# Matmul with rotary embedding on one core: two more pairs of tiles turned on VectorE, and another order of SyncE's loads

## The chip, the core and the metric

The kernel runs on one core of a Trainium2 chip. A core has five engines with their own instruction streams: TensorE (PE, matrix products; PEld in the profile is its weight load), VectorE (DVE), ScalarE (ACT), GpSimd (POOL) and SyncE (SP), which only starts transfers here. They meet through semaphores. Products land in PSUM; everything else lies in SBUF. Transfers between the chip's main memory and SBUF are started by SyncE, ScalarE or GpSimd, each with a queue of its own, and all queues are served by the same sixteen DMA engines.

The metric is the time of one execution in device microseconds; less is better. Before the change the median of 3 runs was 150.48 us (150.37 to 150.66).

## What is computed

```python
batch, seq, hidden, n_heads = (16, 512, 768, 12)      # x: 16 x 512 x 768, weight: 768 x 768
...
y = np.matmul(x, weight)
y = y.reshape(batch, seq, n_heads, head_dim)           # head_dim = 64
...
out1 = y1 * cos1 - y2 * sin1                           # y1, y2: halves of each head
out2 = y2 * cos2 + y1 * sin2
out = np.concatenate([out1, out2], axis=-1)
```

All inputs and the output are float32. The kernel multiplies in float16 and adds up in float32.

## The kernel before

**Tiles and groups.** The 8,192 rows of x are 64 tiles of 128 rows. Four tiles of four different batches that share their rows of cos and sin form a group; there are 16 groups (0 to 15), and tile i is in group i // 4. A group has two halves of two tiles each; a half is named (group, 0) or (group, 1). `NTILE` is 64, `QB` is 4 and `LAST` is 15.

**From x to the product.** PE needs each tile with the contraction along the partitions, so every tile must be transposed. There are two ways.

- A *plain* tile: `load` (L209) brings 128 rows of 3,072 bytes to one of ten buffers `xs` on SyncE's queue; `cast` on ScalarE makes float16 (`xc`, L189); PE transposes it with the identity into PSUM in 12 small products (`turn_rows`, L270); ScalarE copies the result to SBUF (`xt`, L189).
- A *block pair*: two tiles of a half go together, and PE doesn't transpose. `load_quarter` (L224) fetches four quarters, each 32 partitions by 8 rows by 192 values, so in rows of 768 bytes, already spread as the transposed layout needs. VectorE then turns blocks of 32 x 32 (`turn_pair`, L298, a STREAM_TRANSPOSE into `xp`). A pair marked "pool" is loaded by GpSimd's queue, which casts on the way (`xh`). A pair marked "sp" is loaded by SyncE in float32 (one of three buffers `xb`), and ScalarE casts the whole pair (`cast_pair`, L189, into one of two buffers `xd`).

`BLOCKS` (L140 to L142) lists the block pairs: the second halves of groups 4 to 13, ten pairs, "pool" in even groups and "sp" in odd ones.

**From product to output.** PE multiplies with the weight in row halves of 64 partitions (`walk` and `one`, L359) into six PSUM banks: three for a half of a group. VectorE multiplies each finished stretch with cos and sin at once (`rope`, L416; a half has one product of 128 x 1024 and one of 128 x 2048 results, both into `tq` or into the weight's former buffer `w_raw`), GpSimd adds the two parts (`add`, L442) into `ov`, and the result is stored from ScalarE's queue, at the end also from SyncE's (`store`, L474). Groups 14 and 15 go in smaller stretches; in the last one PE, VectorE and ScalarE take some additions.

**Order.** Each engine's order is written out by the loop over tiles (i from 4 to 63). At tile i, ScalarE casts up to five tiles ahead (`casts`, `C_AHEAD`), PE transposes up to three tiles ahead (`turns`, `T_AHEAD`), VectorE turns pairs whose first tile is less than four ahead (`bturns`), GpSimd issues loads up to 20 ahead (`pool_loads`). Every engine takes its instructions strictly in this order, so a wait holds all that stands behind it on that engine.

SyncE's order is the list `fetch`. `pump` issues from it as long as a buffer is free by the plan's count: a tile load needs one of the ten `xs`, a pair's first quarter one of the three `xb`. Before, the quarters of an "sp" pair are entered one by one behind plain tiles from the group ahead of the pair on:

```python
for i in range(QB, NTILE):
    if soon and i >= max(2, soon[0][0] - 1) * QB:
        quarters += [(soon[0], q) for q in (0, 2, 1, 3)]
```

Of the kernel before, what the change touches and what calls it, by code (L numbers as in the profile page):

```python
# [108 lines left out]
def kernel(  # L109
# [23 lines left out]
    QB = 4  # L133
    NG = B * SB // QB
    NTILE = QB * NG
# [4 lines left out]
    BLOCKS = {}  # L140
    for g in range(4, 14):
        BLOCKS[g, 1] = "pool" if g % 2 == 0 and g >= 4 else "sp"  # L142

    def sbuf(name, shape, dt):
        return nc.alloc_sbuf_tensor(name, shape, dt).ap()
# [50 lines left out]
    def pair_of(i):  # L196
        return i // QB, (i % QB) // 2

    def is_block(i):
        return pair_of(i) in BLOCKS  # L200
# [293 lines left out]
        out=sin_sb, in_=sin.rearrange("(p r) d -> p r d", r=SB)), writes=["sin"], dma="ov3_1536")  # L494


    fetch, quarters = [], []
    soon = [p for p in sorted(BLOCKS) if BLOCKS[p] == "sp"]
    for i in range(QB, NTILE):
        if soon and i >= max(2, soon[0][0] - 1) * QB:  # L500
            quarters += [(soon[0], q) for q in (0, 2, 1, 3)]
            soon.pop(0)
        if not is_block(i):
            fetch.append(i)
            if quarters:
                fetch.append(quarters.pop(0))
        elif quarters and quarters[0][0] == pair_of(i):
            fetch.append(quarters.pop(0))
    fetched = [0]
    xs_used, xb_used = [0], [0]  # L510
    xs_sent, xb_sent = [4], [0]
# [1 line left out]
    def pump():  # L513

        while fetched[0] < len(fetch):
            j = fetch[fetched[0]]
            if isinstance(j, int):
                if xs_sent[0] - xs_used[0] >= NX:
                    return
                load(j)  # L520
                xs_sent[0] += 1
            else:
                if j[1] == 0:
                    if xb_sent[0] - xb_used[0] >= NB:
                        return
                    xb_sent[0] += 1
                load_quarter(*j)
            fetched[0] += 1
# [45 lines left out]
    for c in CHUNKS[3:5]:  # L574
# [6 lines left out]
    do("dve", lambda eng: eng.tensor_scalar_mul(  # L581
        out=csn[:, 1, :, HD:D], in0=sin_sb[:, :, 0:HD], scalar1=-1.0),
        reads=["sin", "csn1", "cos"], writes=["csn"])
    assert not quarters
    pump()

    rows_on = [False]
# [42 lines left out]
    for g in range(LAST):  # L630
        for h in (0, 2):
            i = QB * (g + 1) + h
            q = (g, h * H, (h + 2) * H, "act")
# [4 lines left out]
            elif g < LAST - 2:  # L638
                i = QB * (LAST - 2) + 2 * (g - LAST + 4) + h // 2
            else:  # L640
                q = q[:3] + ("sp",)
# [22 lines left out]
    for i in range(QB, NTILE):  # L664
        g, s = divmod(i, QB)
# [13 lines left out]
        for n, p in enumerate(pieces(g, s)) if i >= ROWS else ():  # L679
            a, z, _, bank = p  # L680
# [66 lines left out]
```

## Time and profile before

| | us |
|---|---|
| median of 3 runs | 150.48 |
| the profiled execution, its own time | 150.94 |
| its span, first to last instruction | 149.1 |
| busy in the span: DVE / ACT / POOL | 126.0 / 77.9 / 123.2 |
| PE's transposes in row halves, 38 tiles in 456 products, busy | 15.4 |
| DVE's transposes of pairs: 5 from `xh`, 5 from `xd` | 6.2, 4.8 |
| ScalarE's pair casts, 5 | 8.2 |
| median from issue to landing: tile load / SyncE's quarter | 15.7 / 18.0 |

The profile is of one execution; its span leaves out the start and the end of the launch, so it is compared with that execution's own time. An engine's row gives the time it was busy. The chain of waits follows the work that ended last back through what released it. In the timeline the first column is the start and the second the duration of one or several like instructions; the brackets give the idle time ahead of them and who ended it. The share of the DMA engines can be above 1, because the records of packets on one engine overlap.

### The profile page before, as it was taken

What the parts mean: (1) busy time and instruction counts of PE and PEld (TensorE: products, weight loads), DVE (VectorE), ACT (ScalarE), POOL (GpSimd) and SP (SyncE); (2) the same over time, 40 slices, a digit from 0 to 9 for tenths busy, and PEclk for the clock granted to TensorE, in tenths of its full rate; (3) what the DMA queues carried; (4) which work ended last, traced back from release to release, by engine and by line L of the source; (5) the groups of instructions that cost most, each with busy time, mean ns of one, the idle gap of its engine ahead of it and who ended that gap; (6) DMA issues with size and microseconds to landing.
All of it is one profiled execution on the core that took longest, in us unless ns stands there. A gap on an engine that the chain in (4) does not pass through costs nothing.

```text
span 149.1 us, 4412 instructions
## 1 busy us (share of the span) xinstructions
PE 141.2 (95%) x1948; PEld 116.0 (78%) x1948; DVE 126.0 (84%) x96; ACT 77.9 (52%) x93; POOL 123.2 (83%) x72
## 2 busy tenths in 40 slices
PE   6759999999999999999999999999999999999990
PEld 2325568889888889888888888888888888864870
DVE  0244998884999999899999998999989998898990
ACT  3444698877761833547261915275263817764200
POOL 1000389999999999999999999779895999999990
PEclk9999999999999999999999999999999999999998
DMA  4999999999999999999999999999999999985574
GB/s 122 356 401 401 400 401 399 271 366 324 329 350 339 327 339 356 271 368 349 348 358 367 380 324 357 368 403 323 388 412 411 413 406 405 394 328 218 222 294 160
DMA packets 27555, 51.27 MB, mean 344 GB/s; under 512 B 7184, under 2 KB 13072, under 8 KB 27536
## 3 DMA queue, kind: packets, MB, share of 16 engines
q1 hardware_dynamic: 14736, 28.05, 54.2%
q10 hardware_dynamic: 7360, 20.97, 35.5%
q0 software_dynamic: 5440, 1.97, 10.7%
q8 instruction: 15, 0.25, 0.6%
q14 instruction: 4, 0.03, 0.1%
HBM read 27.79 MB, written 25.17 MB: 355 GB/s over the span
## 4 chain that ended last, share of the span: by engine, by line
PE 85%; DVE 6%; DMA 5%; SPq 1%; issue 1%; DVEq 0%
PE py L359 70%; PE py L334 8%; PE pt L270 5%; DMA w_raw<-in_weight_dram 5%; DVE tq L416 5%; SPq L209 1%; PE pt L255 1%; SPq L231 1%; DVE xs L416 1%; DVE w_sb L189 0%; DVE ov L442 0%; DVEq L57 0%; SPq L742 0%; SPq L119 0%
## 5 line engine op out<-in xcount | busy, mean ns | idle before, releaser
L442 POOL TENSOR_TENSOR ov<-tq 128x1536 f32<-128x1536 f32 (+3 forms) x32 | 76.4, 2412 | 19.4 <-DVE tq L416 19.2
L416 DVE TENSOR_TENSOR tq<-py,csn 128x1024 f32<-128x1024 f32 (+2 forms) x49 | 74.5, 1552 | 4.7 <-PE py L359 3.6
L359 PE MATMUL py<-w_sb,xt 64*128 64x512 f16 (+1 forms) x816 | 77.9, 323 | 0.0
L359 PEld LDWEIGHTS py<-w_sb,xt 64*128 64x128 f16 x816 | 59.2, 94 | 8.4 <-DVE tq L416 0.4
L189 ACT COPY xt<-pt 128x768 f16<-128x768 f16 x42 | 33.5, 799 | 51.7 <-PE pt L270 50.5
L359 PE MATMUL py<-w_sb,xp 64*128 64x512 f16 (+1 forms) x480 | 47.6, 323 | 0.0
L189 ACT CAST xc<-xs 128x768 f16<-128x768 f32 x44 | 38.8, 906 | 9.0 <-DMA xs<-in_x_dram 8.8
L359 PEld LDWEIGHTS py<-w_sb,xp 64*128 64x128 f16 x480 | 35.4, 94 | 4.5
L416 DVE TENSOR_TENSOR w_raw<-py,csn 128x1024 f32<-128x1024 f32 (+1 forms) x21 | 35.1, 1674 | 4.3 <-POOL w_raw L691 2.1
L442 POOL TENSOR_TENSOR ov<-w_raw 128x1536 f32<-128x1536 f32 (+2 forms) x13 | 35.1, 2718 | 2.0 <-DVE w_raw L416 1.8
L334 PE MATMUL py<-w_sb,xt 128*128 128x256 f16 (+2 forms) x132 | 20.1, 302 | 1.9 <-DVE w_sb L189 1.9
L334 PEld LDWEIGHTS py<-w_sb,xt 128*128 128x128 f16 x132 | 11.6, 98 | 8.1 <-DVE w_sb L189 3.3
L270 PEld LDWEIGHTS pt<-ident,xc 64*128 64x128 f16 x456 | 14.8, 95 | 1.7 <-ACT xc L189 0.6
L270 PE MATMUL pt<-ident,xc 64*128 64x64 f16 x456 | 15.4, 190 | 0.0
L224 POOL DMA_DIRECT2D xh<-in_x_dram x20 | 11.6, 588 | 0.0
L189 ACT CAST xd<-xb 128x1536 f16<-128x1536 f32 x5 | 8.2, 1638 | 0.0
L189 DVE CAST w_sb<-w_raw 128x768 f16<-128x768 f32 x6 | 3.4, 560 | 4.4 <-DMA w_raw<-in_weight_dram 4.4
L298 DVE STREAM_TRANSPOSE xp<-xh 128x768 f32<-128x768 f32 x5 | 6.2, 1237 | 0.0
L536 PE MATMUL py<-cold 128*128 128x512 f16 x12 | 4.4, 528 | 1.4 <-DVE cold L479 1.4
L189 DVE COPY xt<-pt 128x768 f16<-128x768 f16 x2 | 1.1, 558 | 4.8 <-PE pt L255 4.8
L298 DVE STREAM_TRANSPOSE xp<-xd 128x768 f32<-128x768 f32 x5 | 4.8, 969 | 0.0
L536 PEld LDWEIGHTS py<-cold 128*128 128x128 f16 x12 | 1.4, 129 | 3.5 <-issue 1.9
(21 smaller groups left out, 15.7 us busy)
## 6 DMA issues: line engine op xcount, KB each, us to landing
out_dram<-ov ACTq DMA_DIRECT2D x26, 768.0 KB, 9.0
xs<-in_x_dram SPq DMA_DIRECT2D x44, 384.0 KB, 15.7
xb<-in_x_dram SPq DMA_DIRECT2D x20, 192.0 KB, 18.0
out_dram<-ov SPq DMA_DIRECT2D x4, 768.0 KB, 3.7
w_raw<-in_weight_dram SPq DMA_DIRECT2D x6, 384.0 KB, 7.8
xh<-in_x_dram POOLq DMA_DIRECT2D x20, 96.0 KB, 14.5
out_dram<-ov SPq DMA_DIRECT2D x1, 384.0 KB, 2.3
out_dram<-ov ACTq DMA_DIRECT2D x1, 384.0 KB, 2.3
```

The costliest lines, as they stand in the source:

```text
L189: eng.copy(out=o, in_=i_) if e == "act" else eng.tensor_copy(out=o, in_=i_)
L209: do(e, lambda eng: eng.dma_start(out=xs_b[k], in_=x[b].rearrange("(p r) h -> r p h", r=SB)[r]), writes=[f"xs{k}"], dma=f"xs{k}")
L224: do(e, lambda eng: eng.dma_start(out=dst[ts(q, R)], in_=src[r, q]), writes=[f"{name}q{q}"], dma=name)
L231: do(e, lambda eng: eng.dma_start(out=w_raw[:, t, h], in_=wv[t, h]), writes=[f"wr{t}{h}"], dma=f"ov{t}_0" if h else f"xb{t}")
L255: do("pe", lambda eng: eng.transpose(pt[:, t, h, :], src[:, t, h, :], ident), reads=[f"xc{c}", "ident"], writes=[f"pt{k}"], tick=(t, h) == ...
L270: do("pe", lambda eng: eng.transpose(pts[r][:, t, h, :], src[rows, t, h, :], ident[rows, rows]), reads=[f"xc{c}", "ident"], writes=[f"pt{r ...
L298: do("dve", lambda eng: eng.transpose(out=dst, in_=src), reads=rd, writes=[f"xp{z}"])
L334: do("pe", lambda eng: eng.matmul(ps, get(t, h), w_sb[:, t, h, a - s * H : z - s * H], start=start, stop=stop), reads=[key, f"w{t}{h}"], w ...
L359: do("pe", lambda eng: eng.matmul(py[:, a:z], get(t, h)[rows], w_sb[rows, t, h, a - s * H : z - s * H], start=start, stop=not opens and en ...
L416: do("dve", lambda eng: eng.tensor_tensor(out=tq.rearrange("p j (h d) -> p j h d", d=D), in0=ps.rearrange("p (h d) -> p h d", d=D) .unsque ...
L442: do(adder, lambda eng: eng.tensor_tensor(out=ov_b[o][:, ds(c0, w)].rearrange("p (h t d) -> p h t d", t=2, d=HD), in0=tq[:, 0].rearrange(" ...
L536: do("pe", lambda eng: eng.matmul(py[:, ts(b, 512)], cold[:, 0:P], cold, start=True, stop=warmed[0] < WARM - 6), reads=["cold"], writes=[f ...
```

## The change

Two pairs become block pairs, the first halves of groups 9 and 12, that is tiles 36, 37, 48 and 49; both are "sp". In these two groups all four tiles are now in block pairs. And `fetch` is built anew: the plain tiles in order, and each quarter of an "sp" pair right behind one of the last four plain tiles ahead of the pair.

```diff
     for g in range(4, 14):
         BLOCKS[g, 1] = "pool" if g % 2 == 0 and g >= 4 else "sp"
+    for g in (9, 12):
+        BLOCKS[g, 0] = "sp"
...
-    fetch, quarters = [], []
-    soon = [p for p in sorted(BLOCKS) if BLOCKS[p] == "sp"]
-    for i in range(QB, NTILE):
-        if soon and i >= max(2, soon[0][0] - 1) * QB:
-            quarters += [(soon[0], q) for q in (0, 2, 1, 3)]
-            soon.pop(0)
-        if not is_block(i):
-            fetch.append(i)
-            if quarters:
-                fetch.append(quarters.pop(0))
-        elif quarters and quarters[0][0] == pair_of(i):
-            fetch.append(quarters.pop(0))
+    plain = [i for i in range(QB, NTILE) if not is_block(i)]
+    fetch = [(i, i) for i in plain]
+    for gh in sorted(BLOCKS):
+        if BLOCKS[gh] == "sp":
+            behind = [i for i in plain if i < gh[0] * QB + 2 * gh[1]][-4:]
+            fetch += [(i + 0.5, (gh, q)) for i, q in zip(behind, (0, 2, 1, 3))]
+    fetch = [what for _, what in sorted(fetch, key=lambda p: p[0])]
...
-    assert not quarters
```

From tile 28 on SyncE's order is then (Q is a quarter, named by its pair):

```
before: 28 Q(7,1) 29 Q(7,1) 32 Q(9,1) 33 Q(9,1) 36 Q(9,1) 37 Q(9,1) 40 Q(11,1) 41 Q(11,1) 44 Q(11,1) 45 Q(11,1) 48 Q(13,1) 49 Q(13,1) 52 Q(13,1) 53 Q(13,1) 56 ...
after:  28 Q(7,1) Q(9,0) Q(9,1)  29 Q(7,1) Q(9,0) Q(9,1)  32 Q(9,0) Q(9,1)  33 Q(9,0) Q(9,1)
        40 Q(11,1) Q(12,0)  41 Q(11,1) Q(12,0)  44 Q(11,1) Q(12,0) Q(13,1)  45 Q(11,1) Q(12,0) Q(13,1)  52 Q(13,1)  53 Q(13,1)  56 ...
```

## The prediction

> **What bounds the kernel now.** I read the busy shares first, then the stretches of the span with the DMA share, then the chain of waits, then ScalarE's and VectorE's own order in time.
>
> ```profile
> PE 141.2 (95%) x1948; PEld 116.0 (78%) x1948; DVE 126.0 (84%) x96; ACT 77.9 (52%) x93; POOL 123.2 (83%) x72
> ```
>
> The stretches (columns: length, then busy time of PE, PEld, DVE, ACT, POOL, granted clock, DMA share, GB/s):
>
> ```profile
> 24.00:60.00 36.00, 36.00 (x573) 31.84 (x571) 31.76 (x19) 22.69 (x29) 35.71 (x22) 1.00 1.13 337
> 60.00:94.00 34.00, 34.00 (x502) 30.14 (x499) 32.22 (x21) 16.50 (x20) 33.54 (x18) 1.00 1.12 347
> 94.00:124.00 30.00, 30.00 (x442) 26.52 (x438) 28.98 (x20) 15.10 (x17) 25.98 (x9) 1.00 1.04 392
> ```
>
> PE has no gap from 24 to 124 us, so PE sets the pace. But the DMA share is above 1: the sixteen DMA engines are full all that time, and the loads have no lead to give away. ScalarE's order and the chain show it for tiles 44 and 45 (casts at 92.52 and 94.03, PE's transposes of the same tiles at 97.58 and 99.68):
>
> ```profile
> 92.52 0.90 ACT L189 CAST xc<-xs 128x768 f16<-128x768 f32 x1
> 94.03 0.91 ACT L189 CAST xc<-xs 128x768 f16<-128x768 f32 x1 [0.60 <-DMA xs<-in_x_dram]
> 97.85 0.80 ACT L189 COPY xt<-pt 128x768 f16<-128x768 f16 x1 [2.92 <-PE pt L270]
> 98.55 1.64 ACT L189 CAST xd<-xb 128x1536 f16<-128x1536 f32 x1
> ...
> 100.07 0.81 ACT L189 COPY xt<-pt 128x768 f16<-128x768 f16 x1
> ```
>
> ```profile
> 97.58 0.16 PE pt L270 x9
> 97.75 0.03 PE py L359
> 97.78 0.03 PE pt L270
> 97.80 1.88 PE py L359 x18
> 99.68 0.19 PE pt L270 x10
> ```
>
> Tile 45's cast waits for its load (0.60 us); what still hides that is the time from the end of the cast (94.94) to PE's first transpose of the tile (99.5 in the order of PE): 4.6 us.
>
> The other near bounds are DVE and POOL:
>
> ```profile
> 101.11 1.23 DVE L416 TENSOR_TENSOR tq<-py,csn 128x1024 f32<-128x1024 f32 x1
> 102.25 0.97 DVE L298 STREAM_TRANSPOSE xp<-xd 128x768 f32<-128x768 f32 x1
> 103.15 5.58 DVE L416 TENSOR_TENSOR tq<-py,csn 128x2048 f32<-128x2048 f32 x3
> 109.26 1.23 DVE L416 TENSOR_TENSOR w_raw<-py,csn 128x1024 f32<-128x1024 f32 x1 [0.54 <-PE py L359]
> 110.41 1.23 DVE L298 STREAM_TRANSPOSE xp<-xh 128x768 f32<-128x768 f32 x1
> 111.56 2.25 DVE L416 TENSOR_TENSOR w_raw<-py,csn 128x2048 f32<-128x2048 f32 x1
> ```
>
> ```profile
> 113.95 3.47 POOL L442 TENSOR_TENSOR ov<-w_raw 128x1536 f32<-128x1536 f32 x1 [1.51 <-DVE w_raw L416]
> 117.37 7.06 POOL L442 TENSOR_TENSOR ov<-tq 128x1536 f32<-128x1536 f32 x3
> ```
>
> DVE idles about 0.5 us a group. POOL is released at 113.95 and from there has no idle time until its last addition ends at 145.40, 0.3 us ahead of DVE's last (145.69): whatever delays that release delays the end.
>
> **Sum, part by part.** *Removed from PE:* the transposes of four tiles (36, 37, 48, 49). On the chain one tile costs 0.16 to 0.19 us, 0.35 to 0.36 a pair, 0.72 in all. *Removed from ScalarE:* four casts (906 ns) and four copies (799 ns), against two pair casts (1,638 ns); ScalarE is half idle and this is worth nothing by itself.
>
> *Added to DVE:* two transposes of 969 ns (the row that reads a ScalarE cast); start to start they take 0.90. DVE has 2.95 us of idle time between 92 and 137.4, so on PE's clock they mostly hide. Where they don't: from the 1,024-wide product at 101.11 to the end of the 2,048-wide one that releases POOL, DVE's steps are 1.14 + 0.90 + 2.17 + 1.15 + 2.17 + 1.15 + 1.15 + 2.25 = 12.08, and the new transpose of (12, 0) falls into it: 12.98. That ends at 114.09 instead of 113.81 if its start keeps, +0.28 us; were that cover gone, both in full: 1.8 us.
>
> *Moved on SyncE's queue:* 44 tile loads become 40, and 20 quarters become 28. The issues (0.43 us each when not held up) are hidden, for SyncE already sits behind a full queue (5.32 us on one quarter at 26.86). The bytes are equal, the DMA time isn't. The packets' records of the trace give a median of 124 ns for a loaded row of 3,072 bytes, 121 for a stored one and 49 for a row of 768, so a tile is 128 x 124 / 16 = 0.99 us of all sixteen engines, a quarter 256 x 49 / 16 = 0.78, and a pair of tiles costs 3.12 as a block instead of 1.98. Two pairs: 2.3 us more, in a stretch where the engines are full.
>
> The order counts more. Both pairs of group 9 now follow tiles 28, 29, 32 and 33, and those of (11, 1), (12, 0) and in part (13, 1) follow tiles 40, 41, 44 and 45, so that two or three quarters stand where one stood. SyncE's queue lands in order, and the other queues' demand stays (stores at PE's pace), so I read off when this queue had moved the same amount before. Issue plus time to landing gives, before: tile 28 at 53.5, tile 37 at 74.3, the quarter behind it at 77.4, tile 49 with the quarter behind it at 102.3.
> - Tile 33 now has 3 tiles and 8 quarters from tile 28 on: 2.97 + 6.24 = 9.21 us of DMA time. Before, 8.85 were done at 74.3 and 9.63 at 77.4. So it lands at 75.7 (before: 65.1).
> - Tile 45 has 7 tiles and 17 quarters: 20.19. Before, 11 and 12, 20.25, were done at 102.3. So it lands at about 102.2 (before: 94.0).
>
> PE transposes tile 33 at 75.07. ScalarE stands at its cast until 75.7, casts for 0.9, and only then copies out tile 32, which must leave PSUM first (0.7): PE goes on at 77.3, 2.2 us late. At tile 45 PE is due at 99.5 + 2.2 - 0.36 = 101.4. Stores and PE are then 2.2 us late as well; the store queue takes 1.94 us of DMA time (256 x 121 / 16) twice in a group of 8.13, or 48%, so loads gain 1.05 us of DMA time and tile 45 lands at about 100.1; with 0.9 and 0.7, PE goes on at 101.7, another 0.3 late. Thus PE is 2.2 - 0.36 + 0.3 = 2.1 us late after tile 45, and POOL's release 2.1 + 0.28 = 2.4 us. PE itself gets another 0.36 back at tiles 48 and 49, which POOL's unbroken run to the end doesn't pass on.
>
> New waits on SyncE: the first quarter of (9, 1) takes the buffer of (5, 1), whose cast ends at 51.3, some 12 us after SyncE gets there; tile 29 and the last quarter of (7, 1) stand behind it. The first of (12, 0) waits in the same way for the cast of (9, 0), at about 80, with tiles 41 to 45 behind. Queued DMAs reach to 57 and 84.6 by then, so I cost both at nothing; without that cover it is the third rival.
>
> Sum against the profiled execution: 150.94 us, span 149.1 (1.8 lie around it). 150.94 + 2.4 = 153.3. It stands 0.46 over the median of 150.48, so the median becomes **152.9**.
>
> The unknown is what a quarter costs in a full queue. Low end: half a tile, by its bytes (0.49). High end: queues take turns by packet, and against stores 256 turns of (49 + 121) / 16 = 2.7 us stand against 1.96 for a tile, 1.4 tiles or 1.37 us. I take 0.78, the packets' own record. At the high end tile 33 needs 2.97 + 10.96 = 13.9, which on the same scale was done at 78.8: PE 5.3 us late, the median at about 156. At the low end there is no stall (next).
>
> **Rivals.**
> 1. *Loads in time (not slower).* If short rows move at the pace of long ones, tile 33 needs 2.97 + 3.92 = 6.9 (before, 6.4 were done at 71.7 and 7.4 at 74.3): 73.0, ahead of the 74.2 at which its cast must start. Tile 45 needs 15.3, done at 98.3; it is due at 97.6 (99.16 less 0.9 and 0.7), and the store that ScalarE's wait holds back leaves the loads up to 1.94 us of DMA time, so I count it as in time. No stall follows; PE gains 0.72 us, but POOL's release moves by only 0.28 - 0.36 = -0.08. Time 150.4 (to 149.8 if the tail follows PE). It decides at a quarter of about 0.5 to 0.6 us. For it: the bytes are equal and 4.6 us of slack lie at tile 45. Against it: 49 ns is 40% of 124, not 25%. The Trainium skill speaks for it (DMA: Bandwidth & Descriptors, Specifications: rows of 512 bytes and more move at line rate); by that rule the sum would be 150.4, and the packets' records here disagree.
> 2. *DVE becomes the bound.* Both transposes in full, 1.8 us, reach POOL's release: 152.3. Against: its 0.5 us of idle time in each group.
> 3. *SyncE's queue runs dry* behind the wait for the cast of (9, 0). If ScalarE is late, some 4 us of loading are lost ahead of tiles 41 to 45: about +5.5, 156.
>
> **How the numbers follow.** Forecast 0.58 (151.3 to 154.8), rival 1 0.26, rival 2 0.07, rival 3 0.09. About 0.3 us (0.2%) is what can be told from no change: rival 1 splits into 0.13 faster and 0.13 same; the rest is slower, 0.74. Range 150.1 to 156.0: it leaves out the far ends of rivals 1 and 3.
>
> **What would show it.** Right: ScalarE's casts of tiles 32/33 and 44/45 wait for their loads by several us, PE shows idle time ended by ScalarE's xc or xt near 75 and 100, the shares of DMA stay above 1 there, and POOL's unbroken run starts near 116.4. Wrong: PE without a gap to 136.6, and an end at -0.1 to -0.7; or PE gaps ended by DVE.

## The result, and the profile after

The changed kernel takes 156.73 us (median of 5, 156.11 to 158.28); the kernel before took 150.37 beside it (149.78 to 150.66). The ratio is 1.0446, with a 95% interval of 1.0381 to 1.0512: 4.5% slower. The profiled execution took 156.37 us, its span 154.6. Ratios here leave out executions more than 1.5% above a kernel's fastest; where a kernel's executions spread wider, all of them are told.

The busy line and the three stretches of the changed kernel (columns as before the change: length, busy time of PE, PEld, DVE, ACT, POOL, granted clock, DMA share, GB/s):

```profile
PE 143.3 (93%) x1900; PEld 110.8 (72%) x1900; DVE 127.9 (83%) x98; ACT 74.9 (48%) x87; POOL 123.1 (80%) x72
```

```profile
24.00:60.00 36.00, 36.00 (x577) 31.26 (x573) 31.69 (x20) 22.27 (x28) 35.72 (x22) 1.00 1.14 333
60.00:94.00 34.00, 30.02 (x379) 23.10 (x376) 27.42 (x19) 11.88 (x12) 27.46 (x15) 0.90 1.13 311
94.00:124.00 30.00, 30.00 (x431) 23.33 (x428) 29.57 (x21) 14.30 (x15) 25.42 (x8) 1.00 1.05 361
```

PE has 48 instructions less and yet 2.1 us more busy time (143.3, before 141.2). PE's own row changed in the middle stretch alone: it idles there for 4 us, and its granted clock is 0.90. VectorE and GpSimd lost 4.8 and 6.1 us of busy time there; they wait for PE.

ScalarE's order in time in the changed kernel (casts of tiles 32, 33; copy of tile 32; casts of tiles 41 and 45):

```profile
68.35 0.91 ACT L191 CAST xc<-xs 128x768 f16<-128x768 f32 x1 [1.33 <-DMA xs<-in_x_dram]
76.38 0.88 ACT L191 CAST xc<-xs 128x768 f16<-128x768 f32 x1 [7.13 <-DMA xs<-in_x_dram]
...
77.16 0.80 ACT L191 COPY xt<-pt 128x768 f16<-128x768 f16 x1
...
91.62 0.91 ACT L191 CAST xc<-xs 128x768 f16<-128x768 f32 x1 [8.49 <-DMA xs<-in_x_dram]
...
101.77 0.90 ACT L191 CAST xc<-xs 128x768 f16<-128x768 f32 x1 [3.23 <-DMA xs<-in_x_dram]
```

PE's order in time around it (the second line is the transposes of tile 33, called T(33) from here on):

```profile
72.30 1.74 PE L361 MATMUL py<-w_sb,xp 64*128 64x512 f16 x17
...
78.01 0.50 PE L272 MATMUL pt<-ident,xc 64*128 64x64 f16 x12 [3.98 <-ACT xt L191]
78.33 4.03 PE L361 MATMUL py<-w_sb,xp 64*128 64x256 f16 x25
...
82.15 0.63 PE L361 MATMUL py<-w_sb,xt 64*128 64x512 f16 x1
```

Before, ScalarE cast tiles 32 and 33 without a wait, the copy of tile 32 came in time, and PE went on to T(33) without idle time:

```profile
68.17 1.73 ACT L189 CAST xc<-xs 128x768 f16<-128x768 f32 x2
73.40 0.80 ACT L189 COPY xt<-pt 128x768 f16<-128x768 f16 x1 [3.51 <-PE pt L270]
75.07 0.35 PE L270 MATMUL pt<-ident,xc 64*128 64x64 f16 x10
```

Now ScalarE stands 7.13 us at the cast of tile 33, which lands at 76.36; the copy of tile 32 is queued behind it, and PE idles for 3.98 us until that copy is done (77.16 + 0.80). That is the predicted wait. What follows was not predicted: the transposes take 0.50 us instead of 0.35, and a product 0.63 instead of 0.38. The stretches of the changed kernel, cut where the granted clock changes, show why:

```profile
72.00:76.45 4.45, 2.03 (x27) 1.41 (x20) 3.06 (x2) 0.07 (x1) 4.33 (x2) 1.00 1.20 285
76.45:79.87 3.42, 1.86 (x23) 1.33 (x25) 0.00 (x0) 2.80 (x4) 3.42 (x4) 0.50 1.09 281
79.87:83.29 3.42, 3.42 (x24) 2.09 (x22) 2.40 (x3) 3.26 (x3) 1.03 (x2) 0.50 1.08 380
83.29:94.00 10.71, 10.71 (x134) 7.90 (x132) 10.24 (x7) 0.91 (x1) 6.92 (x2) 1.00 1.14 310
```

From 76.45 to 83.29 PE had half its clock. It worked from 78.01 on, so it lost (83.29 - 78.01) / 2 = 2.64 us.

**The books.** The steady measure is the time from one tile's transposes to the next one's, for it doesn't depend on when an execution got going. (The profiled executions differ there: T(32) is at 72.95 before and at 71.69 after.)

| from, to | before | after | difference |
|---|---|---|---|
| T(32) to T(33) | 2.12 | 6.32 | +4.20, the wait |
| T(33) to T(40) | 14.18 | 16.40 | +2.22: 2.58 for the clock, less 0.36 for tiles 36 and 37 |
| T(44) to T(45) | 2.13 | 2.12 | 0 |
| T(45) to T(52) | 14.17 | 13.83 | -0.34, tiles 48 and 49 |
| end of PE's last product to end of VectorE's last work | 0.55 | 0.89 | +0.34 |

The first four sum to 6.08 us, and the medians differ by 6.36. POOL's unbroken run now starts at 119.29, 5.3 us later than before and 2.9 later than predicted:

```profile
114.84 3.46 POOL L444 TENSOR_TENSOR ov<-tq 128x1536 f32<-128x1536 f32 x1 [0.72 <-DVE tq L418]
119.29 3.48 POOL L444 TENSOR_TENSOR ov<-w_raw 128x1536 f32<-128x1536 f32 x1 [0.99 <-DVE w_raw L418]
```

### The profile page after: what moved, and what is told of

Same layout as the page of the kernel before. It is cut to its first block, busy times and chain, and to the rows that moved or that the text cites. A ratio compares the mean times of both kernels' runs of the same rounds, so it can differ in the third digit from the quotient of the medians.

```text
span 154.6 us, 4314 instructions
## 1 busy us (share of the span) xinstructions
PE 143.3 (93%) x1900; PEld 110.8 (72%) x1900; DVE 127.9 (83%) x98; ACT 74.9 (48%) x87; POOL 123.1 (80%) x72
## 4 chain that ended last, share of the span: by engine, by line
PE 66%; DMA 15%; SPq 7%; DVE 6%; ACT 2%; issue 1%; DVEq 0%
PE py L361 53%; DMA xs<-in_x_dram 11%; PE py L336 8%; DVE tq L418 4%; SPq L226 4%; DMA w_raw<-in_weight_dram 4%; PE pt L272 4%; SPq L211 2%; ACT xd L191 1%; ACT xt L191 1%; PE pt L257 1%; SPq L233 1%; DVE xs L418 1%; DVE ov L444 1%; DVE w_sb L191 0%
## 5 line engine op out<-in xcount | busy, mean ns | idle before, releaser
L361 PE MATMUL py<-w_sb,xt 64*128 64x256 f16 (+1 forms) x720 | 68.5, 324 | 0.0
L361 PEld LDWEIGHTS py<-w_sb,xt 64*128 64x128 f16 x720 | 50.3, 94 | 10.0 <-issue 0.5
L361 PE MATMUL py<-w_sb,xp 64*128 64x256 f16 (+1 forms) x576 | 56.2, 332 | 0.0
L191 ACT CAST xc<-xs 128x768 f16<-128x768 f32 x40 | 35.7, 905 | 32.6 <-DMA xs<-in_x_dram 32.5
L191 ACT COPY xt<-pt 128x768 f16<-128x768 f16 x38 | 30.3, 800 | 35.2 <-PE pt L272 33.8
L361 PEld LDWEIGHTS py<-w_sb,xp 64*128 64x128 f16 x576 | 39.4, 97 | 10.0 <-issue 0.6
L272 PEld LDWEIGHTS pt<-ident,xc 64*128 64x128 f16 x408 | 13.0, 95 | 6.1 <-ACT xt L191 4.3
L272 PE MATMUL pt<-ident,xc 64*128 64x64 f16 x408 | 13.4, 191 | 4.0 <-ACT xt L191 4.0
L191 ACT CAST xd<-xb 128x1536 f16<-128x1536 f32 x7 | 11.3, 1623 | 0.6 <-DMA xb<-in_x_dram 0.6
L300 DVE STREAM_TRANSPOSE xp<-xd 128x768 f32<-128x768 f32 x7 | 6.7, 963 | 0.0
```

The costliest lines, as they stand in the source:

```text
L191: eng.copy(out=o, in_=i_) if e == "act" else eng.tensor_copy(out=o, in_=i_)
L272: do("pe", lambda eng: eng.transpose(pts[r][:, t, h, :], src[rows, t, h, :], ident[rows, rows]), reads=[f"xc{c}", "ident"], writes=[f"pt{r ...
L300: do("dve", lambda eng: eng.transpose(out=dst, in_=src), reads=rd, writes=[f"xp{z}"])
L361: do("pe", lambda eng: eng.matmul(py[:, a:z], get(t, h)[rows], w_sb[rows, t, h, a - s * H : z - s * H], start=start, stop=not opens and en ...
```

## The experiments

Two questions: is it the two added pairs or the order of the loads that makes tile 33 late; and what does a wait of PE cost, beyond its length? Unless said otherwise the edits are against the changed kernel. They ran in three sets, each beside the kernel before: the first (by casts, filler, four buffers, (12, 0) alone; before 150.77, with one execution of 525.97 left out of the ratios) and the second ((9, 0) alone, (12, 0) with filler, two holds; 150.75) on one chip, the third (ten and eleven pairs by casts, (11, 1) earlier, middle hold; 150.41) on another.

### Is it the order? Twelve pairs in the order of ScalarE's casts

```diff
-    plain = [i for i in range(QB, NTILE) if not is_block(i)]
...
-    fetch = [what for _, what in sorted(fetch, key=lambda p: p[0])]
+    fetch = []
+    for i in range(QB, NTILE):
+        if not is_block(i):
+            fetch.append(i)
+        elif i % 2 == 0 and BLOCKS[pair_of(i)] == "sp":
+            fetch += [(pair_of(i), q) for q in (0, 2, 1, 3)]
```

> All twelve pairs stay; SyncE loads in the order in which ScalarE casts, each pair's four quarters together. Theory (the order made tile 33 late, ScalarE stood at its cast, PE went idle and its clock fell): tile 33 has 3 tiles and 2 quarters from tile 28 on, 4.5 us of DMA time instead of 9.2, and lands near 64 us, tile 45 near 90; PE has no gap; 149.7 to 150.8 us. Rival A (the 2.3 us of DMA time that two more pairs cost is what hurts, whatever the order): 152 or more. Rival B (VectorE, with two more transposes, is the bound): 152 or more, with PE's gaps ended by VectorE.

Measured: ten executions, five from 150.34 to 151.87 and five from 152.71 to 155.11, median 152.29. The ratio, of the first five alone, is 1.0009 (0.9979 to 1.0039). So the same twelve pairs, with the same quarters and VectorE transposes, reach the time of ten pairs in half of the executions: the order of the loads makes most of the loss. But there is nothing to spare. The chain of waits in the profiled execution (151.17 us):

```profile
75.73 24.09 DMA xb<-in_x_dram
...
99.84 0.39 ACT xd L191
100.23 1.13 issue
101.36 0.81 ACT xt L191
...
102.30 3.73 PE py L361 x33
```

The last quarter of (11, 1) takes 24.09 us to land, ScalarE's cast of that pair waits for it, the copy of tile 45 is queued behind the cast, and PE waits 0.65 us. ScalarE's order makes a late load a wait of PE here as at tile 33. Why this quarter took 24.09 us, where the median of this kernel's quarters is 13.8, no run shows.

### Ten and eleven pairs in that order, and one pair a place earlier

```diff
-    for g in (9, 12):
+    for g in ():          # ten pairs; (9,) for eleven
```

> The ten pairs of the kernel before, fetched in the order of ScalarE's casts, a pair's four quarters together: the order alone. Without the two added pairs the DMA engines have 2 x (4 x 0.78 - 2 x 0.99) = 2.3 us less to move ahead of tile 52, so no cast should be late. Theory (the order decides, and this order is safe): 150.3, 150.0 to 150.8, all executions within 0.5 us, TensorE without a wait over 0.5 us after 20 us. Rival (this order of loads is itself unsafe, and that is why the twelve-pair kernel in it spread from 150.3 to 155.1): several executions over 152, as there.

> Eleven pairs, with (9,0), in the order of the casts. TensorE saves the transposes of tiles 36 and 37 (0.36), and the transposes of (12,0) on VectorE, with the 0.2 us that VectorE's end stood behind TensorE's in every kernel with (12,0) against 4.00 without, are not there. Theory (the two pairs cost DMA slack, half as much with one): 150.1, 149.8 to 150.6, with at most one execution over 152. Rival (the quarters of one pair are enough to make tile 45 or the pair (11,1) late): several executions over 152, as with two pairs.

In the third kernel, of twelve pairs, the quarters of (11, 1) are entered ahead of tile 45:

```diff
-            fetch += [(pair_of(i), q) for q in (0, 2, 1, 3)]
+            at_ = len(fetch) - (1 if pair_of(i) == (11, 1) else 0)
+            fetch[at_:at_] = [(pair_of(i), q) for q in (0, 2, 1, 3)]
```

> Twelve pairs in the order of the casts, with the four quarters of (11,1) one place earlier, ahead of tile 45. In the twelve-pair run in this order TensorE waited 0.65 us because ScalarE's cast of (11,1) waited for its last quarter (landing 99.82) ahead of the copy of tile 45, while the load of tile 45 had 4.5 us to spare. Theory (the spread of that kernel comes from this cast): fewer executions over 152 than 5 in 10, fastest near 150.0. Rival (the DMA engines are short of time whatever the order, so the wait moves to tile 45 or to (12,0)): the spread stays, 150.3 to 155, or grows.

| pairs, order | executions | over 152 us | ratio |
|---|---|---|---|
| ten, by casts | 149.90 to 151.03 | 0 of 11 | 0.9999 (0.9976 to 1.0022) |
| eleven with (9, 0), by casts | 149.80 to 151.42; 153.65 to 154.74 | 5 of 11 | 1.0004 (0.9979 to 1.0030) |
| twelve, by casts | 150.34 to 151.87; 152.71 to 155.11 | 5 of 10 | 1.0009 (0.9979 to 1.0039) |
| twelve, (11, 1) a place earlier | 150.65 to 150.98; 153.18 | 1 of 5 | 1.0038 (1.0025 to 1.0051) |

One more execution of the eleven pairs took 189.26 us, with a granted clock of 0.76 over the whole of it; it happened to be the profiled one and is set aside. The order alone changes nothing with ten pairs, as its theory said, though they spread over 1.1 us instead of 0.5. With eleven, the theory's "at most one over 152" fell and the rival held: one added pair is enough to make some executions 3 to 4 us late. Four of those five, and the three slowest of the twelve pairs, have a granted clock of 0.987 to 0.989 over the execution, the others 0.993 or more. The earlier place of (11, 1) seems to help, on five executions, but its ratio stays at 1.0038. No version beats the kernel before. (The 4.00 us in the second of these expectations runs to the last instruction of VectorE's stream, behind the final stores; VectorE's work ends 0.55 us after PE's in the kernel before.) What the late executions wait for was not seen, since none was profiled.

### Four buffers, so that SyncE doesn't wait

```diff
-    NX, NB, NBH, NC, NCP, NXT, NXP, NOV = 10, 3, 3, 5, 2, 8, 4, 4
+    NX, NB, NBH, NC, NCP, NXT, NXP, NOV = 10, 4, 3, 5, 2, 8, 4, 4
```

> The changed kernel with four float32 pair buffers instead of three, so that the first quarters of (9,1) and (12,0) no longer wait for casts of the pairs two and three earlier. Theory (tile 33 is late by the order alone): tile 33 lands within 2 us of 76, PE's idle time there stays 3 to 5 us, 155.5 to 157.5. Rival (SyncE's wait of 12.3 us let its queue run dry, and that cost the time): the wait goes, tiles 41 to 45 land some 5 us earlier, and the time falls to 152.5 or less.

Measured: 157.05 to 159.23, ratio 1.0485 (1.0420 to 1.0551). What SyncE waits for, of the changed kernel and then of this one (total, times, longest):

```profile
SPq L226 <- ACT xd L191: 19.8, 2, 12.3
```

```profile
SPq L226 <- ACT xd L191: 3.6, 1, 3.6
```

The waits for pair casts are nearly gone, and the time is no better (the median of 157.64 is just above the 157.5 expected): tile 33's load, issued at 60.01, still lands only at 78.55, with eight quarters on the way with it. The place in the order makes it late, not SyncE's wait. Of the loads behind that wait, tile 41 lands 6.5 us earlier than in the changed kernel (85.09 instead of 91.60), but tile 45 lands 2.3 later (104.09 instead of 101.75): the wait isn't what makes tile 45 late either.

### Filling PE's wait

```diff
+        if i == 30:
+            for k in range(16):
+                do("pe", lambda eng: eng.matmul(
+                    py[:, 0:512], cold[:, 0:P], cold, start=True, stop=True),
+                    reads=["cold"], writes=["ps0"], tick=False)
         turns(i + 1 + (T_AHEAD if i > QB else 2), 1)
```

> The changed kernel, with 16 products of zeros (512 columns each, some 3.4 us at full clock) on PE ahead of the transposes of tile 33, where it sat idle for 4.0 us; they go to a PSUM bank that is free then. Theory (about half of the loss is PE's clock after the idle time): the wait at tile 33 ends when it did, the clock stays at 1.00 behind it, and the time falls by 2.0 to 2.6 us, to 153.9 to 154.9. Rival (the second half of the loss comes from the late loads of tiles 41 to 45 behind SyncE's wait): no change, 156 to 157.5.

Measured: 157.34 to 159.68, ratio 1.0526 (1.0461 to 1.0591). The expected gain did not come. PE's transposes of tiles 33, 40 and 45 in this kernel:

```profile
78.67 0.35 PE L272 MATMUL pt<-ident,xc 64*128 64x64 f16 x12 [0.66 <-ACT xt L191]
92.50 0.34 PE L272 MATMUL pt<-ident,xc 64*128 64x64 f16 x12
...
105.94 0.35 PE L272 MATMUL pt<-ident,xc 64*128 64x64 f16 x12 [2.90 <-ACT xt L191]
```

The filler did what it was to do: the clock stays at 1.00, and T(33) to T(40) takes 13.83 us, 2.57 less than in the changed kernel. But then PE is at tile 45 before its load, which lands at 104.29, and T(44) to T(45) takes 5.29 instead of 2.12. In the changed kernel PE came to tile 45 later, behind the slow clock, and this second late load cost nothing. So the two losses cover each other, but not in full: the load also lands 2.54 us later here than there (101.75). By the prediction's own argument, that a late PE leaves the loads 48% of its delay in DMA time, some 1.2 us of that are to be expected (an estimate, 48% of 2.57 us); the rest stays open.

### One added pair at a time, and its filler

Eleven pairs, fetched by the changed rule, with (12, 0) alone; then the same with the 16 products ahead of T(45) (`i == 42`):

```diff
-    for g in (9, 12):
+    for g in (12,):
```

> Eleven pairs: (12,0) alone is added, by the changed order rule, which leaves SyncE's order up to tile 41 as it was before the change. Theory: tile 33 lands where it did before (65), no idle time there; tile 45 has three quarters of (12,0) and one of (13,1) more ahead of it (3.1 us of DMA time) and lands at 98 to 100; PE is late by at most 2 us, under the idle time that drops the clock: 150.3 to 152.5. Rival (each added pair costs alike, by DMA time or by VectorE): half the loss, 153 to 154.

> Eleven pairs, with (12,0) alone, as in the run before it, and 16 products of zeros (512 columns each) on TensorE just ahead of its transposes of tile 45, in the place where that run idled for 3.79 us. They fill some 3.5 us of the wait, so the wait for tile 45 stays (landing at about 102, T(45) near 103.7) and TensorE is not idle in it. Theory (the clock falls because TensorE stood idle, and costs (1-0.69)x4 + (1-0.88)x4 = 1.7 us in 102-110 beyond the wait): the clock row stays at 1.00 and the time comes out 1.3 to 2.3 us under the same kernel without filler (156.0), near 154.2. Rival (the loss is the wait alone, or later loads are late as well): no gain, 155.5 to 156.5, as the filler gave none in the twelve-pair kernel.

Measured: (12, 0) alone 155.97 to 158.86, ratio 1.0352 (1.0332 to 1.0372), an expectation missed by 4 us: tile 45 lands at 102.03, and PE idles for 3.79 us ahead of T(45). With filler 154.27 to 156.22, ratio 1.0299 (1.0229 to 1.0368). Stretches of the one without filler, then of the one with it:

```profile
102.00:106.00 4.00, 2.32 (x25) 1.48 (x27) 0.00 (x0) 3.95 (x5) 2.99 (x1) 0.69 1.07 221
106.00:110.00 4.00, 4.00 (x48) 2.97 (x46) 3.57 (x3) 2.99 (x3) 0.00 (x0) 0.88 1.03 339
```

```profile
102.00:106.00 4.00, 3.04 (x42) 1.91 (x41) 0.57 (x1) 3.77 (x5) 2.46 (x1) 1.00 1.07 223
106.00:110.00 4.00, 4.00 (x53) 3.01 (x51) 4.00 (x4) 3.21 (x4) 0.14 (x1) 1.00 1.04 332
```

T(45) comes at 103.68 without and at 103.88 with filler; T(45) to T(52) takes 15.41 and 13.84. So 1.57 us were the clock's. Of the whole time 1.18 arrive between the profiled executions (156.41 and 155.23) and 0.9 between the medians, under the 1.3 to 2.3 expected; the intervals of the two ratios overlap, and the evidence is the trace's.

Then (9, 0) alone, with the changed rule:

```diff
-    for g in (9, 12):
+    for g in (9,):
```

> Eleven pairs, with (9,0) and not (12,0), fetched by the changed rule. Up to tile 33 SyncE's order is that of the changed kernel, so TensorE should stop there as it did (3.98 us idle, ended by ScalarE's copy, T(33) at about 78.0), and its clock row should read about 0.8 in 74-78, 0.5 in 78-82 and 0.84 in 82-86. Theory (a late tile costs its wait, 2.94, and the clock after it, (1-0.50)x4 + (1-0.84)x4 = 2.64, less 0.36 for tiles 36 and 37): 150.4 + 5.2 = 155.6, 154.8 to 156.4. Rival (the second half of the loss comes from the second pair's quarters and SyncE's wait for cast (9,0)): 150.4 + 2.6 = 153.0, 152.3 to 153.6.

Measured: 157.07, 157.60 and 158.88 at a granted clock of 0.978, and 154.33 at 0.999. In the profiled execution (158.88) PE idles for 4.70 us, as tile 33 lands at 79.4. The theory's 155.6 was too low for three of four, in the profiled one because the wait itself was longer; the one execution without a loss of clock is 2.7 us under the next. Either pair alone thus costs nearly the whole loss, and the two don't add up, since behind the first wait PE comes to tile 45 too late to wait for it (T(44) to T(45) is 2.12 in the changed kernel).

### A wait without any change of the loads

The kernel before, with ScalarE held ahead of its copy of tile 32 by copies of zeros: 10, 13, and 12 with a half one. No load is moved.

```diff
+        if i == 29:
+            for _ in range(10):          # 13 in the long hold
+                do("act", copy("act", cold, cold), reads=["cold"], writes=["cold"])
         turns(i + 1 + (T_AHEAD if i > QB else 2), 1)
```

> The kernel before (ten pairs, its own order of loads) with 10 copies of 512 zeros on ScalarE (an estimate of 0.53 to 0.6 us each, from its copy of 768 f16 at 0.80) ahead of its copy of tile 32: no load is moved, TensorE alone is held at T(33). Copy at 75.2 to 75.9, T(33) at 76.1 to 76.8 instead of 75.07, TensorE idle 2.0 to 2.7 us. In the twelve-pair kernel with filler an idle time of 2.90 us left the clock at 1.00, so the theory expects only the delay: +1.0 to +1.7, 151.4 to 152.1. Rival (idle time costs in proportion, as 5.6 for 3.98): +2.8 to +3.8.

> As the short hold, with 13 copies instead of 10: T(33) at 77.7 to 78.5, TensorE idle 3.6 to 4.5 us, as in the changed kernel, with every load where it was. Theory (wait plus clock): the delay of 2.6 to 3.4 and 2.64 for the clock, +5.2 to +6.0, 155.6 to 156.4, and a clock row near 0.8, 0.5, 0.84 behind the wait. Rival (the second half of the changed kernel's loss came from its loads, not from the idle time): +2.6 to +3.4, 153.0 to 153.8, with the clock at 1.00 or its dip without effect on the end.

> The kernel before with ScalarE held ahead of its copy of tile 32 by 12 copies of 512 and one of 256 zeros, 0.3 us less than the long hold: TensorE idle 3.3 to 3.5 us ahead of T(33). It places the idle time from which the clock falls, known so far only to lie between 2.90 (no loss) and 3.68 (1.69 us lost). Theory: a step, so T(33) to T(36) takes either 6.03 us as without a hold or 7.4 to 8.6. Rival (a slope from about 3 us on): something between, 6.4 to 7.2.

Short hold: 152.38 (151.98 to 153.08), ratio 1.0110 (1.0076 to 1.0144). Long hold: 156.46 (156.06 to 156.84), ratio 1.0377 (1.0327 to 1.0427). Middle hold: one execution, 157.13. The short and the long hold come out 0.3 and 0.1 us above the ranges of their theories, and outside those of the rivals. PE's T(33) and what follows, short hold first, then long:

```profile
76.15 0.35 PE L270 MATMUL pt<-ident,xc 64*128 64x64 f16 x12 [1.71 <-ACT xt L189]
76.33 2.12 PE L359 MATMUL py<-w_sb,xp 64*128 64x256 f16 x25
```

```profile
78.74 0.35 PE L270 MATMUL pt<-ident,xc 64*128 64x64 f16 x12 [3.68 <-ACT xt L189]
78.92 3.90 PE L359 MATMUL py<-w_sb,xp 64*128 64x256 f16 x26
```

The same products take 2.12 us behind the short idle time and 3.90 behind the long one. T(32) to T(33) is 1.93 and 3.90 us longer than 2.12; T(33) to T(36), 6.03 before, is 6.03 in the short hold and 7.72 in the long one. So 2 us more of hold cost 4 us more of time, and the changed kernel's loss is there without one load moved: this settles that the second part of it is PE's clock. The stretches of the long and of the middle hold, cut at the changes of the clock:

```profile
75.74:79.15 3.41, 0.41 (x17) 0.39 (x19) 0.40 (x1) 2.85 (x5) 3.29 (x2) 1.00 1.14 341
79.15:82.56 3.41, 3.41 (x27) 2.07 (x24) 1.41 (x2) 2.35 (x3) 2.80 (x5) 0.50 1.10 258
82.56:86.00 3.44, 3.44 (x44) 2.51 (x42) 3.25 (x3) 0.00 (x0) 0.17 (x1) 1.00 1.06 275
```

```profile
74.10:77.52 3.42, 0.50 (x8) 0.14 (x3) 1.56 (x1) 3.26 (x6) 3.31 (x2) 1.00 1.11 358
77.52:80.93 3.41, 2.50 (x27) 1.55 (x29) 0.00 (x0) 2.79 (x5) 3.41 (x5) 0.50 1.12 275
80.93:84.35 3.42, 3.42 (x26) 2.09 (x24) 3.03 (x3) 0.42 (x1) 0.55 (x1) 0.50 1.06 249
84.35:88.00 3.65, 3.65 (x60) 2.89 (x58) 2.84 (x2) 0.25 (x1) 1.89 (x1) 1.00 1.09 333
```

The middle hold was to idle PE for 3.3 to 3.5 us and did so for 3.83, so it doesn't place the threshold as meant. Its T(33) to T(36) takes 8.92 us, above the 7.4 to 8.6 expected of a step: a wait of about the same length can cost one stretch of half clock or two.

## Why the prediction was wrong

- **Direction and mechanism: right.** The place of tile 33 behind eight quarters makes its load late, ScalarE stands at its cast with the copy of tile 32 behind it, and PE stops ahead of T(33).
- **Tile 33's lateness: nearly right.** Predicted landing 75.7, measured 76.36; from landing to T(33) 1.6 us were predicted and 1.65 measured. So the packets' 0.78 us for a quarter fits. By the Trainium skill's rule weighed in the first rival (DMA: Bandwidth & Descriptors, Specifications) tile 33 would have landed at 73.0; the measured landing decides against it here. The term of 2.2 us is 2.94 by T(33) (78.01 against 75.07), and 4.20 from T(32), because the profiled execution of before was 1.26 us late at T(32) and so had less to wait for.
- **The step that failed:** "PE goes on at 77.3, 2.2 us late." The length of the wait was taken for its price. PE goes on at half its clock, and that costs another 2.58 us: two thirds of the miss of 3.8 us (the median of 156.73 against 152.9). Most of the rest is the wait itself, as the line above tells. Neither the sum nor a rival nor a bound of the range had such a term, though PE's idle time was worked out to the tenth of a microsecond. The profile of before could not show the price, as PE's clock is 1.00 in all three stretches there and no idle time is long enough.
- **Tile 45, +0.3:** 0 in the changed kernel. The load came late as predicted (101.75, predicted 100.1), but PE was 5.2 us late by then and did not wait. In the kernel whose PE kept its clock, with the load at 104.29, it cost 3.2 us, much more than predicted.
- **The credits of 0.36 twice:** confirmed, 0.35 (T(33) to T(40) with filler, 13.83 against 14.18) and 0.34.
- **VectorE's added transpose, +0.28:** in order of size. In the profiles of kernels without (12, 0) VectorE's work ends 0.55 to 0.57 us behind PE's (the execution of 189.26 us left aside); with (12, 0) it ends 0.32 to 0.34 later than that in five of seven, 0.13 later in one and no later in one.
- **SyncE's new waits at nothing:** wrong as to what happens, right as to the time so far as it was tried. At the first wait the cover held: loads went on landing up to 59.32, and SyncE issued again at 50.04. At the second it stood for 13.9 us at two quarters, behind the cast of (9, 0), and its queue ran dry, with no landing from 80.93 to 89.78; that is the third rival's mechanism. It made tile 41 late, which PE didn't feel. But four buffers took most of that wait away, and tile 45 and the time were no better.
- **First rival, loads in time:** false for this order of loads, reached by the order of the casts in half of its executions. (By its own measure for tile 45 the cast of tile 33 has to start by 73.5, not 74.2; at 73.0 that changes nothing.) **Second rival, VectorE:** false, as the same transposes are in executions of 150.3 us.
- **Luck:** the third rival and the high end of a quarter's cost both give about 156, near what was measured, but neither holds PE's clock, and the runs show neither to be the cause.

## What to carry to other kernels

Where PE is the bound and its loads land just in time, a late load isn't priced by its wait alone: add what PE's clock costs behind a long idle time, 1.4 to 2.9 us here behind 3.7 us or more, and nothing behind 2.9 us or less. Before loads are regrouped, write down for every load what is due when and what lands ahead of it, for where loads land in the order of issue, as SyncE's did in the kernel before but for two quarters 0.24 us early, one badly placed group becomes a wait of the whole engine chain behind it. And when a filler or a fix at one place brings nothing, look for the next late load, which the first loss had been hiding.

## What the runs showed of the hardware

PE's clock has two levels in these records, 1.00 and 0.50 (only the execution of 189.26 us shows another, 0.75, nearly from end to end), and the half level comes in stretches of one length or twice that:

| kernel | PE idle | half clock | lost, by half of PE's time in it | lost, by the transposes' spacing |
|---|---|---|---|---|
| short hold | 1.71 | none | 0 | 0 |
| filler at T(33), second wait | 2.90 | none | 0 | 0 |
| long hold | 3.68 | 79.15 to 82.56, 3.41 | 1.71 | 1.69 |
| (12, 0) alone | 3.79 | 103.53 to 106.95, 3.42 | 1.63 | 1.60 |
| middle hold | 3.83 | 77.52 to 84.35, 6.83 | 2.96 | 2.89 |
| changed kernel | 3.98 | 76.45 to 83.29, 6.84 | 2.64 | 2.58 |
| (9, 0) alone | 4.70 | 79.04 to 85.87, 6.83 | 2.39 | 2.34 |
| four buffers | 4.98 | 79.56 to 82.98, 3.42 | 1.39 | 1.35 |

The last column compares the time between transposes with that of the kernel before, less 0.36 us where tiles 36 and 37, or 48 and 49, are not transposed.

The price doesn't grow with the idle time. The stretches fit a decision taken every 3.41 us on a raster of its own: in the changed kernel the clock fell 2.4 us after PE went idle (74.03), in the long hold only when PE was at work again. The 3.41 us ahead of a fall hold no work of PE (four buffers, (12, 0) alone) or 0.41, 0.50, 0.76 and 1.00 us of it (long hold, middle hold, (9, 0) alone, changed kernel), and half clock was prolonged by 3.41 us where its first stretch held 2.50 us of work or less, and ended where it held 2.78 or more. The records of the clock bear the raster out: in every trace the times from one change to the next are whole multiples of 3.413 us, for instance 71.68 us or 21 of them between the return of the clock and its last fall in the changed kernel, the long hold, the middle hold and four buffers alike. Laid over the two idle times that cost nothing, the filler kernel's 2.90 us and then the short hold's 1.71, the raster gives

```profile
103.98:107.40 3.42, 1.46 (x28) 1.14 (x30) 0.41 (x1) 3.09 (x4) 3.42 (x2) 1.00 1.07 243
74.13:77.54 3.41, 1.70 (x33) 1.07 (x30) 1.38 (x1) 2.91 (x5) 3.31 (x2) 1.00 1.12 346
```

So the clock fell where a stretch held 1.00 us of work or less, and stayed where it held 1.46 or more. By these rows the work in a stretch decides, and with it where the idle time lies on the raster. No run chose that place: the bounds are read from the rows and were not tried by themselves.

In the profiled executions one stretch of half clock goes with a granted clock of 0.987 to 0.989 over the whole execution, two go with 0.978. So the seven late executions in the order of the casts at 0.987 to 0.989 look like one stretch each.

The Trainium skill states a free-running window of 3,413 ns, and two levels (TensorE: Matmul & The Clock Gate, "What's actually happening"). The lengths agree with 3.41 us here. Its practical rule is to have no idle gaps over some 3.4 us ("HAM oscillation — how this bites in real kernels"). All eight rows agree with it, for the clock stayed up to 2.90 us and fell from 3.68 us on; but the fall came as early as 2.4 us into the idle time, where the stretch still held 1.00 us of work.
